# The last 1 MB of a matmul and RMS norm: four stores of 512 columns on one queue, in the order in which their scaling ends

## The chip, the cores and the metric

The kernel runs on one core of a Trainium2 chip. The metric is the device time of an execution in microseconds (us), as the median of several executions. Every execution also leaves a profile: a span (about 1.8 us shorter than the measured time), engine records and DMA records. In these, PE is TensorE (matmuls), DVE is VectorE, ACT is ScalarE, POOL is GpSimd, and SP is SyncE, which issues DMAs, as ACT does too. A store is moved by the core's 16 DMA engines in packets; here one packet is one unbroken piece of the output, 2 KB for 512 columns and 4 KB for 1024. A store has landed when its last completion event stands in the trace. All times compared below are of executions in the same, undisturbed state unless it is said otherwise.

## The reference

```python
def reference(a, b, gamma, eps):            # a, b: 2048 x 2048 float32
    x = np.matmul(a, b)
    rms = np.sqrt(np.mean(x ** 2, axis=-1, keepdims=True) + eps)
    return (gamma * x / rms).astype(np.float32)
```

A row can be scaled only when the squares of all its 2048 columns have been summed. So the 128 rows computed last can be stored only after the last matmul, and this tail is what the change touches.

## The kernel before

The matmul is done in groups of two row blocks of 128 rows. In the last group, the squares of row block `rb` end with `half_sq`. From them comes the row factor `r_b`, and then the four quarters of the block (512 columns each) are scaled: two on DVE, two on ACT. `xb` holds the left 1024 columns, `right` the right 1024; `HALF` is 1024 and `CH` is 512. This is a cut of the kernel.

```python
        # ... last matmuls, squares ...
        r_b = inverse_rms(half_sq[:, 1:2], part)          # ACT square root, DVE reciprocal
        nc.vector.tensor_scalar_mul(out=xb[:, 0:CH], in0=xb[:, 0:CH], scalar1=r_b)       # DVE
        nc.sync.dma_start(out=rows(rb, 0, CH), in_=xb[:, 0:CH])                          # 256 KB
        by_r(right[:, 0:CH], r_b)                                                        # ACT
        for bank, col in zip(half, halves):
            scaled_gamma(right[:, CH:][:, col], bank, r_b, gam[3][:, col])               # DVE, twice
        nc.sync.dma_start(out=rows(rb, HALF, N), in_=right)                              # 512 KB
        by_r(xb[:, CH:], r_b)                                                            # ACT
        nc.scalar.dma_start(out=rows(rb, CH, HALF), in_=xb[:, CH:])                      # 256 KB
```

`rows(rb, lo, hi)` is `out[rb*128:(rb+1)*128, lo:hi]`. The output has rows of 2048 float32, so 8 KB. A store of 512 columns therefore writes 128 pieces of 2 KB that lie 8 KB apart, and a store of 1024 columns 128 pieces of 4 KB that lie 8 KB apart.

## Time and profile before

| | |
|---|---|
| time, median of 3 runs | 221.41 us (221.40 to 221.79) |
| span of the profiled run | 219.9 us |
| PE busy | 95% |
| start of the last reciprocal (`r_b`) | 213.76 us |
| from there to the last byte, to the last completion, to the end of the span | 4.51, 5.07, 6.15 us |

The first lines of the page of the kernel before: the busy time of each engine.

```profile
span 219.9 us, 3044 instructions
...
PE 209.3 (95%) x1032; PEld 97.4 (44%) x1032; DVE 165.9 (75%) x326; ACT 127.0 (58%) x263; POOL 36.3 (16%) x75
```

The body is bound by TensorE. The tail is not: its last matmul begins 1.2 us before the reciprocal. The timeline of the kernel before, from the last reciprocal on (start in us, length in us, engine, line, operation; SPq and ACTq are issues of DMAs):

```profile
213.76 0.16 DVE L346 RECIPROCAL r<-rms 128x1 f32<-128x1 f32 x1 [0.50 <-ACT rms L352]
213.96 0.72 ACT L729 ACTIVATE a<-a,r 128x512 f32<-128x512 f32 x1 [0.23 <-DVE r L346]
213.96 0.49 DVE L799 TENSOR_SCALAR x<-x,r 128x512 f32<-128x512 f32 x1
214.36 0.87 DVE L725 SCALAR_TENSOR_TENSOR a<-acc,r,gamma_sb 128x256 f32<-128x256 f32 x2
214.47 0.33 SPq L800 DMA_DIRECT2D out_dram<-x  x1
214.58 0.71 ACT L729 ACTIVATE x<-x,r 128x512 f32<-128x512 f32 x1
215.29 0.33 SPq L804 DMA_DIRECT2D out_dram<-a  x1
215.32 0.36 ACTq L806 DMA_DIRECT2D out_dram<-x  x1
```

The three stores are issued 0.71, 1.53 and 1.56 us after the reciprocal began. The next view cuts the time into half microseconds, beginning 1.5 us after the reciprocal. Each line has the stretch, its length, the busy time (and instructions) of PE, PEld (weight loads), DVE, ACT and POOL, and the granted TensorE clock. The last two columns are the mean busy share of the core's 16 DMA engines and what they moved in GB/s; a packet is counted whole in the stretch in which it begins, so a share can exceed 1:

```profile
215.26:215.76 0.50, 0.00 (x0) 0.00 (x0) 0.00 (x0) 0.03 (x1) 0.00 (x0) 1.00 0.92 348
215.76:216.26 0.50, 0.00 (x0) 0.00 (x0) 0.00 (x0) 0.00 (x0) 0.00 (x0) 0.99 0.85 299
216.26:216.76 0.50, 0.00 (x0) 0.00 (x0) 0.00 (x0) 0.00 (x0) 0.00 (x0) 0.50 0.93 360
216.76:217.26 0.50, 0.00 (x0) 0.00 (x0) 0.00 (x0) 0.00 (x0) 0.00 (x0) 0.50 1.06 426
217.26:217.76 0.50, 0.00 (x0) 0.00 (x0) 0.00 (x0) 0.00 (x0) 0.00 (x0) 0.50 1.04 401
217.76:218.26 0.50, 0.00 (x0) 0.00 (x0) 0.00 (x0) 0.00 (x0) 0.00 (x0) 0.50 0.73 262
```

So no compute engine works after 215.3 us, and the DMA engines move 1 MB. There is a small hole (0.85) between the first store and the second.

### The profile page before, as it was taken

What the parts mean: (1) busy time and instruction counts of PE and PEld (TensorE: products, weight loads), DVE (VectorE), ACT (ScalarE), POOL (GpSimd) and SP (SyncE); (2) the same over time, 40 slices, a digit from 0 to 9 for tenths busy, and PEclk for the clock granted to TensorE, in tenths of its full rate; (3) what the DMA queues carried; (4) which work ended last, traced back from release to release, by engine and by line L of the source; (5) the groups of instructions that cost most, each with busy time, mean ns of one, the idle gap of its engine ahead of it and who ended that gap; (6) DMA issues with size and microseconds to landing.
All of it is one profiled execution on the core that took longest, in us unless ns stands there. A gap on an engine that the chain in (4) does not pass through costs nothing.

```text
span 219.9 us, 3044 instructions
## 1 busy us (share of the span) xinstructions
PE 209.3 (95%) x1032; PEld 97.4 (44%) x1032; DVE 165.9 (75%) x326; ACT 127.0 (58%) x263; POOL 36.3 (16%) x75
## 2 busy tenths in 40 slices
PE   7799999999999999999999999999999999999970
PEld 3344544444454444444444444444444444444440
DVE  1128799999889999979795639946695659787781
ACT  2110002920599898688745997289747996334471
POOL 7544443343020002100200002000200000000040
PEclk9999999999999999999999999999999999999996
DMA  7999999999929895948799049965699249145045
GB/s 157 164 203 206 199 206 208 212 206 228 409 76 362 291 293 118 358 176 230 213 300 405 3 93 265 351 247 95 156 294 405 42 100 364 73 174 210 1 171 212
DMA packets 36864, 46.60 MB, mean 212 GB/s; under 512 B 22256, under 2 KB 26352, under 8 KB 35568
## 3 DMA queue, kind: packets, MB, share of 16 engines
q0 software_dynamic: 10608, 23.86, 44.1%
q1 hardware_dynamic: 25824, 22.02, 33.5%
q10 hardware_dynamic: 416, 0.52, 0.7%
q8 instruction: 8, 0.13, 0.2%
q14 instruction: 8, 0.07, 0.1%
HBM read 34.60 MB, written 16.78 MB: 234 GB/s over the span
## 4 chain that ended last, share of the span: by engine, by line
PE 65%; DMA 23%; ACT 4%; POOL 2%; issue 1%; DVE 1%; ACTq 0%; POOLq 0%
PE acc L285 64%; DMA b<-in_b_dram 14%; DMA early<-in_a_dram 5%; DMA a<-in_a_dram 4%; ACT sq L219 2%; POOL b L102 1%; ACT at_even L192 1%; PE acc L790 1%; POOL early L106 1%; DVE s L260 1%; DVE at_even L192 0%; ACT x L729 0%; DVE x L551 0%; ACT norm L222 0%; ACT x L531 0%
## 5 line engine op out<-in xcount | busy, mean ns | idle before, releaser
L285 PE MATMUL acc<-b,s 128*128 128x512 bf16 x408 | 93.3, 379 | 0.5 <-DVE s L260 0.5
L285 PEld LDWEIGHTS <-s 128*128 128x128 f16 (+1 forms) x512 | 49.9, 98 | 60.4 <-DVE s L260 1.0
L388 PE MATMUL acc<-b,head_at 128*128 128x512 bf16 x176 | 43.2, 379 | 1.2 <-DMA b<-in_b_dram 1.2
L303 ACT ACTIVATE sq<-x 128x512 bf16<-128x512 f32 x53 | 33.4, 630 | 6.9 <-DVE x L722 3.0
L370 DVE SCALAR_TENSOR_TENSOR x<-x,r,gamma_sb 128x1024 f32<-128x1024 f32 x28 | 34.8, 1282 | 0.7
L219 ACT ACTIVATE sq<-a 128x1024 bf16<-128x1024 f32 x24 | 25.3, 1053 | 2.1 <-DMA a<-in_a_dram 1.5
L388 PEld LDWEIGHTS <-head_at 128*128 128x128 bf16 x176 | 16.9, 98 | 20.6 <-issue 1.6
L242 ACT ACTIVATE head_at<-a,s 128x2048 f16<-128x2048 f32 x10 | 20.0, 1998 | 3.3 <-DVE s L229 3.3
L102 POOL DMA_DIRECT2D b<-in_b_dram x32 | 17.2, 540 | 20.8 <-DMA b<-in_b_dram 15.0
L430 ACT COPY x<-acc 128x512 f32<-128x512 f32 x5 | 2.9, 582 | 24.7 <-PE acc L388 24.7
L285 PEld LDWEIGHTS <-head_at 128*128 128x128 f16 (+1 forms) x112 | 10.9, 98 | 13.2
L285 PE MATMUL acc<-early,head_at 128*128 128x512 bf16 x64 | 14.5, 379 | 0.0
L285 PEld LDWEIGHTS <-at_even 128*128 128x128 f16 x96 | 9.4, 98 | 11.3
L285 PE MATMUL acc<-early,s 128*128 128x512 bf16 x56 | 14.2, 379 | 0.0
L260 DVE TENSOR_TENSOR s<-head_at 128x1024 f16<-128x1024 f16 (+5 forms) x22 | 13.4, 635 | 0.1
L609 DVE TENSOR_TENSOR x<-x,x 128x512 f32<-128x512 f32 x9 | 6.2, 692 | 8.8 <-ACT x L607 8.3
L127 POOL COPY pace<-x 128x1 f32<-128x1 f32 x4 | 1.7, 413 | 66.7 <-DVE x L618 65.6
L591 ACT COPY x<-acc 128x512 f32<-128x512 f32 x9 | 5.2, 573 | 11.5 <-PE acc L285 11.5
L173 DVE COPY head_at<-tbank 128x1024 bf16<-128x1024 bf16 x7 | 4.8, 692 | 8.7 <-PE tbank L168 8.5
L285 PE MATMUL acc<-t_left,s 128*128 128x512 bf16 x48 | 11.3, 379 | 0.0
L774 POOL TENSOR_SCALAR x<-x,r 128x512 f32<-128x512 f32 x1 | 2.7, 2652 | 51.2 <-DVE r L346 51.2
L276 DVE TENSOR_TENSOR b<-b 128x1024 bf16<-128x1024 bf16 x16 | 10.8, 684 | 0.2
(113 smaller groups left out, 237.5 us busy)
## 6 DMA issues: line engine op xcount, KB each, us to landing
out_dram<-x SPq DMA_DIRECT2D x29, 512.0 KB, 3.8
a<-in_a_dram POOLq DMA_DIRECT2D x10, 1024.0 KB, 8.7
b<-in_b_dram POOLq DMA_DIRECT2D x32, 256.0 KB, 10.0
a<-in_a_dram POOLq DMA_DIRECT2D x4, 512.0 KB, 9.8
early<-in_a_dram POOLq DMA_DIRECT2D x7, 256.0 KB, 10.2
gamma_sb<-in_gamma_dram POOLq DMA_DIRECT2D x2, 512.0 KB, 8.3
out_dram<-x SPq DMA_DIRECT2D x3, 256.0 KB, 2.6
out_dram<-a SPq DMA_DIRECT2D x1, 512.0 KB, 3.3
```

The lines of the kernel that those rows point to most:

```text
L102: nc.gpsimd.dma_start(out=raw[j][kp][:, t, :], in_=b[lo:lo + P, j * HALF:(j + 1) * HALF])
L173: nc.vector.tensor_copy(out=head_at[:, 2 * kp:2 * kp + 2, :, :], in_=view)
L219: nc.scalar.activation(out=junk, in_=a32[mb][:, h * HALF:(h + 1) * HALF], func=ACTF.Square, scale=2.0 ** -8, accum_out=n2[:, h:h + 1])
L242: nc.scalar.activation(out=a16[mb], in_=a32.pop(mb), func=ACTF.Copy, scale=factor.pop(mb))
L260: nc.vector.tensor_tensor(out=sum_of(g, s)[:, lo:hi, :], in0=x[:, lo:hi, :], in1=y[:, lo:hi, :], op=op)
L276: nc.vector.tensor_tensor(out=flat[:, 1:3, :], in0=flat[:, 1:3, :], in1=flat[:, 0::3, :], op=ALU.add)
L285: nc.tensor.matmul(bank, lhsT[:, kp, :], rhs, start=(start and kp == 0), stop=(kp == KP - 1), skip_group_check=not start)
L303: nc.scalar.activation(out=sq[:, 0:CH], in_=src, func=ACTF.Square, scale=inv_sqrt_n, accum_out=msq[mb][:, c:c + 1])
L370: nc.vector.scalar_tensor_tensor(out=x, in0=x, scalar=inverse_of[mb], in1=gamma_sb[:, h * HALF:(h + 1) * HALF], op0=ALU.mult, op1=ALU.mult)
L388: nc.tensor.matmul(bank, head_at[:, kt, r, :], head_rhs(c, kt), start=(kt == 0), stop=(kt == KT - 1))
L591: nc.scalar.copy(out=c, in_=one[1])
L609: nc.vector.tensor_tensor(out=t, in0=t, in1=x12, op=ALU.add)
```

## The change

Its intent: `right`'s first 512 columns are scaled at 214.68 us but wait until 215.23 for DVE to finish the other half. The change stores each quarter as soon as it is scaled, in that order, and puts all four on SP's queue.

```diff
         nc.sync.dma_start(out=rows(rb, 0, CH), in_=xb[:, 0:CH])
         by_r(right[:, 0:CH], r_b)
+        nc.sync.dma_start(out=rows(rb, HALF, HALF + CH), in_=right[:, 0:CH])
         for bank, col in zip(half, halves):
             scaled_gamma(right[:, CH:][:, col], bank, r_b, gam[3][:, col])
-        nc.sync.dma_start(out=rows(rb, HALF, N), in_=right)
         by_r(xb[:, CH:], r_b)
-        nc.scalar.dma_start(out=rows(rb, CH, HALF), in_=xb[:, CH:])
+        nc.sync.dma_start(out=rows(rb, HALF + CH, N), in_=right[:, CH:])
+        nc.sync.dma_start(out=rows(rb, CH, HALF), in_=xb[:, CH:])
```

## The prediction

> **What bounds the kernel now.** The page gives PE 95% busy over a span of 219.9 us, so the body is bound by TensorE. Compared instruction by instruction, the two programs agree on PE, DVE and POOL; ACT loses its last issue, and SP ends with four issues instead of two. Only the tail after the last matmul (about 212.8 us in the chain of waits) can move.
>
> **The tail before (timeline, window after 213.9 us).** The row factor is ready at 213.9. Then in parallel: DVE 128x512 scaling 213.96 to 214.45 and two 128x256 products 214.36 to 215.23; ACT two scalings of 0.72 and 0.71 us, ending 214.68 and 215.29. Issues, each 0.33 us on SP: 256 KB at 214.47, 512 KB at 215.29, and 256 KB on ACT at 215.32 (0.36 us). The packet records show the first store's data on the DMA engines from about 215.3, the last byte at 218.28, the last completion at 218.82; the span ends 1.1 us later with the closing barrier. So the tail is DMA: 1 MB in about 2.95 us. In half-microsecond windows the DMA share is 0.94 to 1.05, but 0.87 in 216.0 to 216.5, where the first store has ended and the second's data has not begun (near silence at 216.1 to 216.2).
>
> **What the change does.**
> - Removes: the wait of right's first 512 columns (scaled by 214.68) for DVE's end at 215.23. Its store can issue as soon as SP has finished its first issue (214.80), about 214.85. By the issue-to-data delay of the first store (0.8 to 0.9 us), data comes at about 215.7, before the first store's data ends at 216.1: the gap closes.
> - Adds: a serial issue on SP. Stores now issue at about 214.47, 214.86, 215.29 and 215.68 (0.33 us each plus about 0.06 us). The last is 0.36 us later than ACT's was, but its data is ready by about 216.6, while the DMA engines have queued bytes until about 217.4: hidden.
> - Adds: smaller rows. Packets of 4096 B took 161 ns, of 2048 B 86 ns (medians of the packet records), so 512 KB cost 8 x 161 = 1.29 us per engine and now 16 x 86 = 1.38 us: +0.09 us. The Trainium skill, "DMA: Bandwidth & Descriptors", section "Why small descriptors are slow (HBM only)", says each packet carries a fixed overhead; these two durations agree in sign.
> - Nothing is gained from one queue as such: that page, "Issuing engines are not separate DMA queues", says that SP and ACT issues share the same 16 engines; the trace agrees (both queues' packets interleave from 216.6 at the same total rate).
>
> **Sum.** An estimate from these: 32 packets x 86 ns = 2.75 us of unbroken data from about 215.33 gives a last byte at 218.1 instead of 218.28, last completion near 218.65, span about 219.7. All of it is on the critical path, but it is 0.15 to 0.2 us of 221.4; the three runs before already differ by 0.4 us.
>
> **Predicted:** 221.25 us, eight times in ten between 220.9 and 221.6. Chances: faster by over 2% 0.01, within 2% 0.98, slower by over 2% 0.01.
>
> **What would show it right or wrong.** Right: the second store issues near 214.85 and the DMA share has no dip near 216.1; the fourth issues near 215.7 with data waiting already; last completion 0.1 to 0.25 us earlier. Wrong: SP's issues space out beyond 0.4 us, so that the fourth store's data comes after the third's end; completions on one queue lag more behind the last byte than the 0.55 us seen; or the smaller packets take longer than 86 ns when all four stores queue. Each would turn the small gain into a loss of some tenths of a microsecond, still within 2%.

## The result, and the profile after

The changed kernel took 221.90 us (median of 6 runs, 221.59 to 222.50), the kernel before 221.59 us in 6 runs (221.40 to 221.86). The ratio is 1.0017, with an interval of 1.0000 to 1.0033: the same at 2%, but on the other side of 1 from the prediction, and above its range.

The timeline of the changed kernel, same part as before. All of it stands 0.49 us later than in the trace before, because this execution reached the tail later (see the first pair of experiments); so compare differences from the reciprocal.

```profile
214.25 0.16 DVE L346 RECIPROCAL r<-rms 128x1 f32<-128x1 f32 x1 [0.50 <-ACT rms L352]
...
214.96 0.33 SPq L800 DMA_DIRECT2D out_dram<-x  x1
215.07 0.70 ACT L729 ACTIVATE x<-x,r 128x512 f32<-128x512 f32 x1
215.38 0.38 SPq L802 DMA_DIRECT2D out_dram<-a  x1
215.86 0.41 SPq L806 DMA_DIRECT2D out_dram<-a  x1
216.36 0.40 SPq L807 DMA_DIRECT2D out_dram<-x  x1
```

The issues stand at 0.71, 1.13, 1.61 and 2.11 us after the reciprocal. The second store left early, as intended. Now the half microseconds of the changed kernel, again from 1.5 us after the reciprocal:

```profile
215.75:216.25 0.50, 0.00 (x0) 0.00 (x0) 0.00 (x0) 0.03 (x1) 0.00 (x0) 1.00 0.93 348
216.25:216.75 0.50, 0.00 (x0) 0.00 (x0) 0.00 (x0) 0.00 (x0) 0.00 (x0) 1.00 1.03 369
216.75:217.25 0.50, 0.00 (x0) 0.00 (x0) 0.00 (x0) 0.00 (x0) 0.00 (x0) 1.00 1.03 320
217.25:217.75 0.50, 0.00 (x0) 0.00 (x0) 0.00 (x0) 0.00 (x0) 0.00 (x0) 1.00 1.12 295
217.75:218.25 0.50, 0.00 (x0) 0.00 (x0) 0.00 (x0) 0.00 (x0) 0.00 (x0) 1.00 1.00 361
218.25:218.75 0.50, 0.00 (x0) 0.00 (x0) 0.00 (x0) 0.00 (x0) 0.00 (x0) 0.66 0.96 295
218.75:219.25 0.50, 0.00 (x0) 0.00 (x0) 0.00 (x0) 0.00 (x0) 0.00 (x0) 0.50 0.31 115
```

Read the two last columns together. The hole is gone (1.03 instead of 0.85 in the second line). But from the third line to the sixth the engines are busy (0.96 to 1.12) and move only 295 to 361 GB/s, in three of the four lines at most 320, where before they moved 360 to 426 in the third to the fifth. A busy share of 1 with fewer bytes means that each packet takes longer. The packet records of the trace say so: the mean of a 2048 B packet is 98.2 ns, against 88.1 ns before. The median did not move (85 and 86 ns); some packets take up to 200 ns. For one engine, 32 packets of that mean are 3.14 us instead of the 2.75 us predicted. And then the engines did not end together: the 16 completion events of the last store spread over 0.76 us (0.33 us for the last store before).

### The profile page after: what moved, and what is told of

Its sections match the earlier page's. It is cut to its first block, busy times and chain, and to the rows that moved or that the text cites. A ratio compares the mean times of both kernels' runs of the same rounds, so it can differ in the third digit from the quotient of the medians.

```text
span 220.7 us, 3046 instructions
## 1 busy us (share of the span) xinstructions
PE 210.3 (95%) x1032; PEld 98.2 (44%) x1032; DVE 165.7 (75%) x326; ACT 127.1 (58%) x263; POOL 36.4 (16%) x75
## 4 chain that ended last, share of the span: by engine, by line
PE 65%; DMA 26%; ACT 4%; DVE 1%; issue 1%; ACTq 0%; POOLq 0%
PE acc L285 64%; DMA b<-in_b_dram 17%; DMA early<-in_a_dram 5%; DMA a<-in_a_dram 4%; ACT sq L219 2%; ACT at_even L192 1%; PE acc L790 1%; DVE s L260 1%; DVE at_even L192 0%; ACT a L729 0%; ACTq L842 0%; DVE x L551 0%; ACT norm L222 0%; ACT x L531 0%; ACT sq L793 0%
```

## The experiments

Two theories could explain the longer tail. *Serial issue*: SP's issues stretched to 0.38 to 0.41 us, so the fourth store left 0.55 us later than the last one had. *Stretched packets*: something about four short-row stores makes their packets slow. A third possibility was that the trace was an outlier. This table has all kernels in the order of the text; the times are from the start of the last reciprocal, from the traces' packet records and semaphore events. Each store leaves 16 completion events, which I take to be one for each DMA engine; "15 of 16" is the time by which every store had 15 of its 16.

| kernel | reciprocal at | last byte | 15 of 16 | last completion | end of span | mean ns of a packet (2 KB / 4 KB) |
|---|---|---|---|---|---|---|
| before | 213.76 | 4.51 | 5.03 | 5.07 | 6.15 | 88.1 / 166.2 |
| before, again (b2) | 213.85 | 4.75 | 5.02 | 5.23 | 6.31 | 87.6 / 166.1 |
| change | 214.25 | 4.95 | 5.48 | 5.49 | 6.48 | 98.2 |
| change, again (a2) | 214.00 | 4.88 | 5.46 | 5.46 | 6.44 | 97.7 |
| split | 212.93 | 5.02 | 5.37 | 5.69 | 6.66 | 93.6 |
| queue | 213.46 | 4.59 | 5.29 | 5.30 | 6.35 | 87.6 / 164.5 |
| long_last | 213.31 | 4.77 | 5.20 | 5.24 | 6.27 | 94.3 / 185.0 |
| packed (slow) | 570.40 | 4.43 | 4.78 | 4.78 | 5.75 | 86.8 |
| packed2 | 213.42 | 4.43 | 4.78 | 4.79 | 5.78 | 86.9 |
| pairs | 213.17 | 4.53 | 4.87 | 4.88 | 5.99 | 163.5 (4 KB) |
| pairs_again | 213.42 | 4.59 | 4.87 | 4.92 | 6.03 | 163.3 (4 KB) |
| pairs2 | 215.55 | 4.62 | 4.76 | 4.95 | 6.03 | 163.6 (4 KB) |

### Both kernels again: b2 and a2

No edit.

> The kernel before, again, as a control: ratio 1.000 within 0.0015, and a second trace of its tail. From the reciprocal of the last row block to the last completion the first trace has 5.06 us (213.76 to 218.82), to the end of the span 6.15 us. If these repeat within 0.1 us, tails of single traces can be compared; if they scatter by 0.3 us, they cannot.

> The changed kernel, again. Its first trace has 5.49 us from that reciprocal to the last completion and 6.47 us to the end. Theory 'the tail is really longer': 5.4 to 5.6 us again, ratio about 1.0015. Theory 'that trace was an outlier' (it was the slowest of six runs, and it began the tail 0.49 us later): 4.8 to 5.0 us as predicted, ratio 0.999.

The unchanged kernel against itself gave a ratio of 1.0017 (interval 0.9994 to 1.0039), median 221.97 us. The change gave 1.0006 (0.9987 to 1.0026), median 221.68 us. So a ratio of 1.0017 over the whole execution tells nothing here: the very same program produces it. My control missed its own expectation of 0.0015 narrowly.

The tails do tell something. The change repeats to 0.03 us (5.49, 5.46), the kernel before to 0.16 us (5.07, 5.23), and the two pairs stand apart. The 0.16 us lie between the 0.1 and the 0.3 us that I had named, and they are one completion event: by 15 of 16 the kernel before repeats to 0.01 us (5.03, 5.02) and the change to 0.02 us (5.48, 5.46), and the two are 0.43 to 0.46 us apart. In each of these eleven traces (packed is left aside) one event of the store issued just before the reciprocal, at line 779, also comes late, at 2.05 to 3.02 us, when its other 15 are in by 1.92. It comes latest in split (3.02) and b2 (2.66), and there the tail's very last event lags most behind the rest (0.32 and 0.21 us). One engine with leftover work would explain this; it was not tested. So the "15 of 16" column is the steadier measure of a tail. The scatter of whole executions comes from earlier. One mark shows it: the subtraction on DVE at line 551 began between 65.83 and 67.15 us, depending on the execution, and from there to the last reciprocal it was 147.10 us, to the hundredth, in ten traces (before, b2, the change, a2, split, queue, long_last, packed2, pairs, pairs_again; pairs2 took 149.53 us). In these ten, everything that differs up to the tail is thus laid down in the first 67 us. The tail has to be read from its own start.

### The split alone, and the queue alone

```diff
 split, against the change
-        nc.sync.dma_start(out=rows(rb, CH, HALF), in_=xb[:, CH:])
+        nc.scalar.dma_start(out=rows(rb, CH, HALF), in_=xb[:, CH:])
 queue, against the kernel before
-        nc.scalar.dma_start(out=rows(rb, CH, HALF), in_=xb[:, CH:])
+        nc.sync.dma_start(out=rows(rb, CH, HALF), in_=xb[:, CH:])
```

> The split alone: four stores of 512 columns as in the change, but the last one issued by ACT as before. Theory 'serial issue' (SP's issues stretched to 0.38 to 0.41 us and the fourth left 0.6 us later than ACT's did): tail back to 5.06 us or less, ratio at or below 1.000. Theory 'four short-row stores stretch their packets' (packets of 2048 B took up to 0.2 us instead of 0.086 in the changed kernel, whatever queue): tail stays at 5.4 us or more, ratio about 1.0015.

> The queue alone: the kernel before with its last store moved from ACT to SP, three stores of 512, 1024 and 512 columns. Theory 'serial issue': last issue about 0.4 us later and the tail 5.3 us or more, ratio about 1.001. Theory 'four short-row stores': the queued data hides the later issue, 5.06 us within 0.1, ratio 1.000.

The split with its last store on ACT ends last of all, at 5.69 us, although its last issue came at 1.61 us and not at 2.11. Its last event alone makes it the slowest: by 15 of 16 it stands at 5.37 us, about 0.1 us before the change and 0.34 us after the kernel before. So serial issue is not the main cause: of the change's loss of about 0.44 us, about 0.34 stay with the split when the queue is taken away. The queue alone keeps short packets (87.6 ns) and its last byte comes at 4.59 us, between the two traces of before; yet it completes at 5.30 us (5.29 by 15 of 16, 0.26 us after before). That meets the number that I wrote for serial issue, not the one for short rows, so one queue does cost something here, in the completion and not in the data. It is one trace of each. The ratios were 1.0004 and 1.0001, both indistinguishable from 1. The split is what stretches packets. It was still open why.

### The stores by themselves: stores

A program of stores only, with no matmul and a wrong result. Each pattern runs four times with quiet between; its data is ready beforehand. It was executed once, so its state is unknown, but all patterns stand in the same execution. (The cut below is shortened.)

```diff
+    def as_change(mb):                                  # 2 KB pieces, 8 KB apart, one row block
+        sp(out=rows(mb, one), in_=big[:, one])          # then three, four, two
+    def other_rows(mb):                                 # the same column range of four row blocks
+        sp(out=rows(mb, one), in_=big[:, one])          # then rows(mb - 1, one), ...
+    def contiguous(mb):                                 # each 256 KB into one unbroken piece
+        sp(out=flat(mb, 0), in_=big[:, one])            # then flat(mb, 1), ...
+    ... single, in_order, two_queues, long_middle, halves, whole, spaced
```

> The disputed cost by itself; the result is wrong on purpose (constants are stored, most rows are left). No matmul; data is ready before each pattern, each pattern four times with quiet between. 1 MB in patterns of stores. If short rows alone stretch packets, one 256 KB store already shows over 95 ns per 2048 B packet, and 'contiguous' (the 256 KB in one piece) too. If several short stores in flight from one queue do it, 'single' has 86 ns and 'as_change', 'in_order', 'other_rows', 'contiguous' all have 95 ns or more. If it is where the rows lie in HBM (four column ranges of the same rows), 'other_rows' or 'contiguous' stay at 86 ns while 'as_change' has 98. 'spaced' (issues 0.6 to 0.7 us apart, as fast as the data drains) should be at 86 ns if overlap of stores is the cause, 'two_queues' at least as slow as 'as_change' (the split run had mean 93.6 ns there but a later end). 'long_middle', 'halves', 'whole': 161 ns per 4096 B, and an end 0.3 to 0.5 us before 'as_change'.

| pattern | mean ns of a packet | last completion after the first issue, us |
|---|---|---|
| single (one store of 256 KB) | 86.0 | 2.4 to 2.5 |
| as_change | 97.5 to 99.5 | 4.76 to 4.81 |
| in_order (columns left to right) | 98.4 to 98.5 | 4.79 to 4.82 |
| other_rows | 98.0 to 98.6 | 4.76 to 4.86 |
| contiguous | 86.8 to 87.2 | 4.06 to 4.07, once 4.41 |
| two_queues (SP and ACT) | 98.1 to 99.6 | 4.79 to 4.87 |
| spaced (issues 0.52 us apart) | 98.9 to 99.3 | 4.83 to 4.89 |
| long_middle (256, 512, 256 KB) | 86 (2 KB), 171 to 174 (4 KB) | 4.55 to 4.61 |
| halves (512, 512 KB: 4 KB pieces) | 163 (4 KB) | 3.93 to 3.95 |
| whole (1 MB: 8 KB pieces) | 316 to 317 (8 KB) | 3.84 to 3.85 |

The profile shows it in the time from issue to landing of the fourth store, of `as_change` (L61) and of `contiguous` (L79); the second line shown of each has the minimum, median and maximum in us (the lines between are left out here and in the next such view):

```profile
L61 SPq DMA_DIRECT2D out_dram<-big x4: 447/454/456, 17.2 to 36.9; - x4
DMA to landing us min/median/max: 3.4/3.4/3.5
...
L79 SPq DMA_DIRECT2D out_dram<-big x4: 450/453/460, 98.3 to 115.5; - x4
DMA to landing us min/median/max: 2.7/2.7/3.1
```

The issues are as far apart and as long in both. The sizes, the rows in SBUF, the queue and the number of packets are the same. Only the place of the pieces in memory differs, and it is worth 0.7 us. Neither the order of the columns nor which row block is written matters. The 4.41 us of `contiguous` are one late completion event, in the execution in which an 8 KB packet of instructions (309 ns) fell among the last packets. Expectations were missed too: `long_middle` ended only 0.15 to 0.26 us before `as_change`, with its 4 KB packets stretched, and `halves` and `whole` 0.8 to 1.0 us before it. Two of the patterns did not do what I had written: `spaced` came out 0.52 us apart, still faster than 256 KB drain, so it does not test stores without overlap; and in `two_queues` ACT's two stores went first, since their sources were ready first.

### Which distance, and how many stores: pitch

The same four stores from SP, into scratch tensors whose rows are 2 to 32 KB apart; then 1 to 6 stores into the output.

```diff
+    def stores_at_pitch(pitch):
+        dst = nc.dram_tensor(f"at_{pitch}", (4 * P, pitch), FP32).ap()
+        return [(dst[n * P:(n + 1) * P, 0:CH], big[:, pieces[n]]) for n in range(4)]
```

> Wrong on purpose, no matmul. Four back-to-back stores of 256 KB from SP, rows of 2 KB, into a scratch tensor whose rows lie 2, 4, 6, 8, 10, 12, 16 or 32 KB apart; then 1, 2, 3, 4 and 6 such stores at 8 KB. Theory 'the pitch decides': 2 KB 86.8 ns mean and last completion 4.07 us after the first issue, 8 KB 98 ns and 4.8 us as in the run before; if only large powers of two hurt, 6, 10 and 12 KB are fast; if any gap does, all but 2 KB are slow; if it worsens with the pitch, 16 and 32 KB are over 100 ns. Number of stores: one 86 ns, the excess growing from the second or third on if writes pile up behind the memory.

Here are the landings of the fourth store for rows 2 KB (L68), 4 KB (L76), 8 KB (L92), 10 KB (L100) and 16 KB (L116) apart:

```profile
L68 SPq DMA_DIRECT2D at<-big x3: 449/451/455, 4.4 to 15.9; - x3
DMA to landing us min/median/max: 2.7/2.7/2.7
...
L76 SPq DMA_DIRECT2D at<-big x3: 405/450/452, 21.6 to 33.1; - x3
DMA to landing us min/median/max: 2.7/2.7/2.7
...
L92 SPq DMA_DIRECT2D at<-big x3: 412/452/458, 56.5 to 69.1; - x3
DMA to landing us min/median/max: 3.3/3.3/3.4
...
L100 SPq DMA_DIRECT2D at<-big x3: 392/448/458, 75.4 to 87.0; - x3
DMA to landing us min/median/max: 2.7/2.7/3.0
...
L116 SPq DMA_DIRECT2D at<-big x3: 410/457/457, 110.0 to 121.5; - x3
DMA to landing us min/median/max: 2.7/2.7/2.7
```

Of the eight distances, 8 KB alone is slow: 95.5 to 96.1 ns per packet and a last completion 4.62 to 4.74 us after the first issue. At 2, 4, 6, 10, 12, 16 and 32 KB it is 86.1 to 87.4 ns and 4.05 to 4.07 us (once 4.41, again beside an 8 KB packet of instructions). Each distance was tried in one scratch tensor alone; only 8 KB was seen in two places, here and in the output. None of my three forms of the theory (any gap, large powers of two, worse with distance) had foreseen that. The output of this kernel has rows of exactly 8 KB. The number of stores at 8 KB counts too: the mean packet is 85.9 ns for one store, about 92 ns for two, 99 ns for three, 98 ns for four and 94 ns for six. A single store hides the trouble in its packets, though not in its completion (2.4 us, where the first store of the packed kernel below needs 2.0 us).

### The change with nothing altered but the place: packed and packed2

```diff
+        def piece(n):
+            lo = rb * P + n * (P // 4)
+            return out[lo:lo + P // 4, :].rearrange("r (q c) -> (r q) c", q=4)
-        nc.sync.dma_start(out=rows(rb, 0, CH), in_=xb[:, 0:CH])
+        nc.sync.dma_start(out=piece(0), in_=xb[:, 0:CH])
         ... and piece(1), piece(2), piece(3) for the other three
```

The last row block is permuted, so the result is wrong there.

> The changed kernel with one thing altered: its four last stores have the same sources, issue order and queue, but each writes its 256 KB into one unbroken piece of memory instead of 128 pieces of 2 KB that lie 8 KB apart. The last row block of the result is wrong on purpose (its numbers are permuted). If the spread destination is what stretches the packets: mean 86 to 88 ns instead of 98, last byte about 4.2 and last completion 4.6 to 4.95 us after the reciprocal (the change had 5.46 and 5.49), which is what was predicted for the change. If it is the queue or the number of stores: 98 ns and 5.4 to 5.5 us as in the change. Ratio about 0.999, not measurable.

> The change with unbroken destinations again, because the profiled execution of the first try fell in a state in which the matmuls ran at less than half their pace (576 us). In a normal execution: mean packet 86 to 88 ns, last completion 4.75 to 4.85 us after the reciprocal as in that trace (the change has 5.46 and 5.49) if the spread destination is the cause, 5.4 to 5.5 us if the short tail of that trace came from the slow state.

In the first try the profiled execution ran its matmuls at less than half their pace (span 576 us). (Its five fast runs gave a ratio of 0.9943, 0.9903 to 0.9983, against the runs of the kernel before that spread to 224.25 us; see pairs_again below.) The second has a normal execution. Its half microseconds, from 1.5 us after the reciprocal:

```profile
214.92:215.42 0.50, 0.00 (x0) 0.00 (x0) 0.00 (x0) 0.03 (x1) 0.00 (x0) 0.64 0.92 344
215.42:215.92 0.50, 0.00 (x0) 0.00 (x0) 0.00 (x0) 0.00 (x0) 0.00 (x0) 0.50 1.03 381
215.92:216.42 0.50, 0.00 (x0) 0.00 (x0) 0.00 (x0) 0.00 (x0) 0.00 (x0) 0.50 1.00 369
216.42:216.92 0.50, 0.00 (x0) 0.00 (x0) 0.00 (x0) 0.00 (x0) 0.00 (x0) 0.50 1.02 389
216.92:217.42 0.50, 0.00 (x0) 0.00 (x0) 0.00 (x0) 0.00 (x0) 0.00 (x0) 0.50 1.04 389
217.42:217.92 0.50, 0.00 (x0) 0.00 (x0) 0.00 (x0) 0.00 (x0) 0.00 (x0) 0.50 0.61 225
```

The same busy share as in the changed kernel now carries 369 to 389 GB/s instead of 295 to 361, and the data ends half a microsecond sooner. Its four issues stand at 0.71, 1.14, 1.61 and 2.12 us and last 0.33, 0.38, 0.41 and 0.40 us, as in the change. So the slower issues cost nothing here. With 86.9 ns per packet and a last completion at 4.79 us, this is the tail that the prediction had described (last completion about 4.9 us after the reciprocal). The destination's 8 KB distance is the cause of the longer tail, with everything else in the program held: 4.78 us by 15 of 16 instead of 5.48 and 5.46, and the last store's events spread over 0.18 us instead of 0.76. (packed2 ran on another chip than a2; `stores` has both patterns in one execution, so the chip is not the reason. The expected last byte of 4.2 us was missed, it came at 4.43. The ratio was 1.0014, interval 0.9964 to 1.0064; the tail does not show in it.)

### Two short stores in a row: long_last

```diff
 against the kernel before
         nc.sync.dma_start(out=rows(rb, 0, CH), in_=xb[:, 0:CH])
+        by_r(xb[:, CH:], r_b)
+        nc.sync.dma_start(out=rows(rb, CH, HALF), in_=xb[:, CH:])
         by_r(right[:, 0:CH], r_b)
         ...
         nc.sync.dma_start(out=rows(rb, HALF, N), in_=right)
-        by_r(xb[:, CH:], r_b)
-        nc.scalar.dma_start(out=rows(rb, CH, HALF), in_=xb[:, CH:])
```

> Three stores on SP: 512 columns at 0.71, the neighbouring 512 at about 1.14, then one of 1024 at about 1.6 us. Two short stores stand back to back as in the change, but only two. Theory 'short stores in flight stretch packets': if two suffice, mean of the 2048 B packets over 92 ns and last completion 5.1 us or more; if it takes the row of four, 86 ns, no gap in the data, last completion 4.7 to 4.85 us.

Two suffice: 94.3 ns, and 5.24 us. The 4 KB packets behind them were stretched as well, 185 ns instead of 164 to 166. So the stretch reaches the next store. The ratio was 0.9988 (0.9952 to 1.0023).

### A version without short rows: pairs, pairs_again and pairs2

The left half is scaled first, by DVE and ACT side by side, and then only two stores of 1024 columns are left.

```diff
 pairs, against the kernel before
         nc.vector.tensor_scalar_mul(out=xb[:, 0:CH], in0=xb[:, 0:CH], scalar1=r_b)
-        nc.sync.dma_start(out=rows(rb, 0, CH), in_=xb[:, 0:CH])
+        by_r(xb[:, CH:], r_b)
+        nc.sync.dma_start(out=rows(rb, 0, HALF), in_=xb)
         by_r(right[:, 0:CH], r_b)
         ... the two scaled_gamma ...
         nc.sync.dma_start(out=rows(rb, HALF, N), in_=right)
-        by_r(xb[:, CH:], r_b)
-        nc.scalar.dma_start(out=rows(rb, CH, HALF), in_=xb[:, CH:])
 pairs2, against pairs: DVE takes xb[:, 0:640], ACT xb[:, 640:]
```

> A version meant to beat both: left half first, scaled by DVE and ACT side by side, then two stores of 1024 columns on SP at about 0.98 and 1.55 us after the reciprocal (no short rows). Theory 'short stores in flight stretch their packets': 2 x 8 packets x 161 ns = 2.58 us of data from about 1.65, last byte 4.25 to 4.4, last completion 4.8 to 4.95 us (before 5.07 and 5.23, change 5.46 and 5.49). Theory 'the first store's early start is what counts': 5.3 us or more, as it starts 0.27 us later. Ratio not measurable either way (0.999 to 1.001).

> The version with two stores of 1024 columns, again, for a second trace and more rounds: last completion 4.88 us after the reciprocal within 0.1, ratio 0.998 to 1.000.

> The same with the left half shared out so that its two scalings end together: DVE takes 640 columns, ACT 384, instead of 512 each. By the rates seen (DVE 0.49, ACT 0.71 us per 512) they end at about 0.80 and 0.78 us instead of 0.92, so the first store issues about 0.12 us earlier, at 0.83, and all data follows: last completion 4.74 to 4.8 us if the first store's start sets the end, 4.88 if not.

Half microseconds of pairs, from 1.5 us after its reciprocal:

```profile
214.67:215.17 0.50, 0.00 (x0) 0.00 (x0) 0.00 (x0) 0.03 (x1) 0.00 (x0) 0.88 0.52 209
215.17:215.67 0.50, 0.00 (x0) 0.00 (x0) 0.00 (x0) 0.00 (x0) 0.00 (x0) 0.50 1.01 401
215.67:216.17 0.50, 0.00 (x0) 0.00 (x0) 0.00 (x0) 0.00 (x0) 0.00 (x0) 0.50 1.02 418
216.17:216.67 0.50, 0.00 (x0) 0.00 (x0) 0.00 (x0) 0.00 (x0) 0.00 (x0) 0.50 1.00 402
216.67:217.17 0.50, 0.00 (x0) 0.00 (x0) 0.00 (x0) 0.00 (x0) 0.00 (x0) 0.50 0.99 393
217.17:217.67 0.50, 0.00 (x0) 0.00 (x0) 0.00 (x0) 0.00 (x0) 0.00 (x0) 0.50 0.75 287
```

It starts later (209 GB/s in the first line, where the others had 344 to 348), and then runs at about 400 GB/s without a hole. The last completion is at 4.88 and 4.92 us and the end of the span at 5.99 and 6.03 us: 0.12 to 0.32 us less than the two traces of the kernel before, and 0.41 to 0.49 us less than the change. Its medians were 221.25 and 221.30 us, beside 221.68 and 222.31 us for the kernel before, with ratios of 0.9989 (0.9946 to 1.0031) and 0.9950 (0.9910 to 0.9989). The second ratio missed its expectation of 0.998 to 1.000. In that call the runs of the kernel before spread from 221.31 to 224.25 us, so most of that half percent is their scatter: the tail accounts for a tenth of a percent.

Pairs2 missed by its last completion. Its first store was issued 0.10 us earlier, at 0.84, and yet it ended at 4.95 us. But 15 of the last store's 16 events were in by 4.76 us, 0.11 us before pairs and within the 4.74 to 4.8 us expected; one event came 0.19 us later. Packets of an earlier store were still moving until 1.85 us after the reciprocal, when its own data had begun at 1.67. That would explain the late event, but nothing was run to show it, and in pairs_again they moved until 2.03 us (data from 1.77) and cost only 0.05 us. (Its median was 221.46 us, ratio 0.9964, 0.9920 to 1.0009.)

## Why the prediction was wrong

- *The body is untouched, and the effect is far below 2%.* Right. From the mark at line 551 to the last reciprocal it took 147.10 us in both kernels.
- *The second store issues early and closes the hole.* Right: 1.13 us after the reciprocal (1.09 foreseen), and the DMA share of that half microsecond went from 0.85 to 1.03.
- *SP's issues of 0.33 us plus 0.06.* Wrong: back to back they took 0.38 to 0.41 us, and the fourth came at 2.11 us instead of 1.92. *The delay is hidden by queued bytes*: right for unbroken pieces (packed2 has the same late issues and ended at 4.79 us). With pieces 8 KB apart the data hid it too in queue, but the completion there came 0.71 us after the last byte, more than the 0.55 us that the prediction had named as a sign of being wrong.
- *"32 packets x 86 ns = 2.75 us of unbroken data".* This is the step that failed. The 86 ns came from the kernel before, where no two stores of 512 columns followed each other that closely. In the changed kernel the mean was 98.2 ns, which makes 3.14 us per engine, 0.39 us more than the term of the sum; the engines then ended apart (the last store's completion events spread over 0.76 us), and the last byte came at 4.95 us instead of the 4.34 us predicted. The prediction named this among the things that would prove it wrong ("the smaller packets take longer than 86 ns when all four stores queue"), but gave it no weight. The runs showed the reason: 2 KB pieces that lie 8 KB apart, and several stores of them in flight. With pieces that lie otherwise, the term was right (86.9 ns).
- *Shorter rows cost 0.09 us.* The fixed cost per packet was right in sign and size (2 x 86 against 161 ns), but it is not the cost that counted. The Trainium skill says in "DMA: Bandwidth & Descriptors", section "Why small descriptors are slow (HBM only)", that each packet carries a fixed overhead; `contiguous` has as many packets of the same size, so it can't explain the difference between `contiguous` and `as_change`.
- *Nothing is gained from one queue as such.* Not contradicted: the same page, section "Issuing engines are not separate DMA queues", has both issuers on the same 16 engines. But it was not free. By 15 of 16, one queue ended about 0.1 us after two with the split (5.48 and 5.46 against 5.37) and 0.26 us after without it (5.29 against 5.03 and 5.02). `two_queues` and `as_change` differed by about 0.1 us or less.
- *The range.* Too narrow. It was laid around the median of three runs, 221.41 us. The same program later had medians of 221.55, 221.59, 221.62, 221.68, 221.97 and 222.31 us. Most of the 0.65 us between 221.25 predicted and 221.90 measured is not to be told from this scatter; what the traces show for the tail is 0.13 to 0.33 us more than before (0.43 to 0.46 us by 15 of 16), where about 0.17 us less had been predicted.

What stays open is the mechanism in memory: why 8 KB, and neither 4 nor 16 KB, makes writes of 2 KB slow, while pieces of 4 KB at the same distance hardly suffer among themselves (163 ns in `halves`) and are slower beside 2 KB pieces (171 to 185 ns in `long_middle` and long_last).

## What to carry to other kernels

Splitting a store so that its parts leave earlier also changes what the parts look like in memory, so time the parts with the row distance of the real output and as many in flight as there will be; one isolated store may look fine. When the DMA share stays at 1 and the GB/s fall, look at the destination first; here it was the cause, and the issue was not. Where an effect of a tenth of a percent is in question, measure it in the traces from the last common event, look whether a single late completion makes the end, and run the unchanged kernel against itself before believing a ratio.

## What the Trainium skill lacked or had wrong

- "DMA: Bandwidth & Descriptors", section "Latency and other measured facts", has a row on the distance of HBM rows at large powers of two. It speaks of copies between HBM tensors at 512 KiB and more, and of padding by a few KiB as a cure. Lacking: stores from SBUF of 2 KB rows that lie just 8 KB apart lose too, from the second in flight on (92 to 99 ns per packet instead of 87; four of them end 4.6 to 4.9 us after the first issue instead of 4.05), and here larger powers of two, 16 and 32 KB, did not.
- The same page, section "Anatomy of one DMA — SWDGE (gpsimd) path", says that the completion waits for the receipt of the last byte. In every trace here the completion of a store issued from SP stands after its last byte, and the time between varies: from last byte to last completion 0.36 us for unbroken pieces (packed2) and 0.33 to 0.35 us for 4 KB pieces (pairs), but 0.54 and 0.58 us for the four short-row stores of the change, 0.71 us in queue and 0.78 us for `single`, one short-row store alone.
- "Perfetto Trace Analysis", section "DMA Optimizations", says that splitting DMAs may let some start sooner if the DMA engines are generally idle. These engines were not idle (0.85 to 1.06 busy in the tail before, until its last half microsecond). The same split lengthened the tail with pieces 8 KB apart (5.49 and 5.46 us against 5.07 and 5.23) and shortened it with unbroken ones (4.79), so idleness did not decide here. Lacking is that the parts can become slower (98 ns per packet of 2048 B instead of 88).
- No page that I read gives how back-to-back stores from one issuer lengthen its issues: 0.33 us alone, 0.38 to 0.46 us for the second to fourth, about 0.55 us for the fifth and 0.64 us for the sixth.
